# First layer of a two-layer mixture of experts: experts sorted on the chip by number of tokens, nine places of 128 slots and seven of 64

## The chip, the cores and the metric

The kernel runs on one core of a Trainium2 chip. The metric is the device time of one execution in microseconds (us); less is better. The engines of the core work side by side: TensorE (PE; its weight loads are PEld), VectorE (DVE), ScalarE (ACT), GpSimd (POOL) and SyncE (SP), and 16 DMA engines move data.

## The reference

Two layers over 256 latent and 256 context tokens of width 1024. Each layer has an attention part, which the change does not touch, and a mixture of 16 experts. The first layer runs it for all 512 tokens, the second for the 256 latent tokens. Every token picks one group of four experts and two experts in it:

```
grp = jnp.argmax(lg, -1)
le_sel = jnp.take_along_axis(le, grp[:, None, None], axis=1)[:, 0]
top_v, top_i = lax.top_k(le_sel, TOP_K)
w_top = jax.nn.softmax(top_v, -1) * p_grp
eid = grp[:, None] * EXPERTS_PER_GROUP + top_i
...
for e in range(N_EXPERTS):
    a = jax.nn.silu(hf @ w_gate[e]) * (hf @ w_up[e])
    y = y + gate[:, e:e + 1] * (a @ w_down[e]).astype(jnp.float32)
```

w_gate and w_up of one expert are 1024 x 512, w_down 512 x 1024, all float32: 6 MB per expert, 96 MB per layer. In the first layer 512 tokens make 1024 pairs of token and expert, 64 per expert on the mean.

## The kernel before

**First layer** (`full_experts`, lines 1318 to 1473). After the routing on VectorE (lines 1250 to 1317), `tables` (line 1328) makes for every expert the rows to gather, the rows to scatter and the weights of its 128 slots: VectorE compares the tokens' ranks with the slots' numbers (line 1336), TensorE multiplies with the tokens' records. `expert` (line 1373) gathers the rows from DRAM (`hfD`) by an indirect DMA of GpSimd (line 1376), turns them feature-major on TensorE (line 1386), and multiplies in three float32r passes: rows and weights are split into a high and a low part, and high x high, high x low and low x high are summed (`product`, lines 1369 to 1371). `split_w` (line 1353) splits the weights: ScalarE writes the high part (line 1358), VectorE, for one part in six GpSimd, the low part (line 1360), into ten buffers `hl`. The weighted output goes to `yD` in DRAM by an indirect DMA (line 1426), each token's two experts into two rows. Only the last expert's output stays in PSUM; `combine` and `finish` add it by a one-hot product (line 1672) to the rows of `yD`, which `base` reads back at the start of the second layer (lines 1640 and 1645).

The weights come in tiles of 1 MB, two each of gate, up and down per expert, through a ring of ten places (`RING[0]`), in the order of their use: `todo` (line 1149) holds up of expert e - 1, gate of e, down of e - 1. SyncE issues the loads (line 1135) in this order, each when its place is free. For a big tile that is after its split. Ten tiles are issued before the first split frees a place (`FILL`).

The loop (lines 1464 to 1472) lets the first half of the next expert's gate follow on up, and down follow on the next expert's gate. A scheduler orders the instructions of each engine from this. `overflow` (line 1609) runs further rounds for every expert if a flag says that one has more tokens than slots (line 1298).

**Second layer** (`half_experts`, from line 1475). Its experts have 64 slots. The products are plain float32, not split: a tile of weights goes from the ring straight to TensorE, the left half of the columns on one half of the array and the right half on the other (`ps[64 * t:64 * t + 64]`, lines 1547 and 1564).

Of the kernel before, what the change touches and what calls it, by code (L numbers as in the profile page):

```python
# [7 lines left out]
F32 = mybir.dt.float32  # L8
F32R = mybir.dt.float32r
BF16 = mybir.dt.bfloat16  # L10
# [10 lines left out]
E = 16  # L21
# [7 lines left out]
CAP = (128, 64)  # L29
RAW_A = 2  # L30
# [7 lines left out]
T4 = 6  # L38
LOG = (2, 3, 4, 5, 6, 7)

# column layout of the constant block (all of it follows from shapes alone)
C_ID, C_TRI, C_NAM, C_WIN, C_R64, C_R32, C_IOTA, C_TIE, C_COEF, C_TLOW, C_REV, C_IOTA2, C_END = np.cumsum(
    [0, 128, 128, 64, 256, 256, 128, 128, 4, 8, 1, 128, 128]).tolist()
# [15 lines left out]
def _constants():  # L59
# [15 lines left out]
    # slot records (valid, token in chunk, chunk, k, ...) -> row to gather, row to scatter, less BIG  # L75
    c[:, C_COEF:C_COEF + 8] = [-BIG, 1, 128, 0, -BIG, 1, 128, 512]
    c[:, C_TLOW] = p
# [4 lines left out]
def kern(tc, I, out):  # L82
# [23 lines left out]
    class Phase:  # L106
        """Working pool of a phase: its bytes are reused by the phases after it."""
# [24 lines left out]
    # ------------------------------------------------------------------ constants  # L132
# [9 lines left out]
    # records of the tokens of layer 0: valid, row, chunk, ..., 0; the rest comes with the routing  # L142
# [33 lines left out]
    def load_x():  # L176
        """residual streams: chunks 0, 1 latents, 2, 3 context"""
# [50 lines left out]
    def ln_stats(x):  # L228
        """-mean and 1 / std of the rows of x [128, D]"""
# [9 lines left out]
    def ln_stats2(x, total, tag):  # L239
        """the same where the row sums are there already"""  # L240
# [7 lines left out]
    def stats(x, c, tot, nmean, ss):  # L248
        """column c of -mean, and the sum of the squares about the mean"""
# [4 lines left out]
    def in_order(*engines):  # L254
        """what the block traces on these engines stays in this order"""
# [1503 lines left out]
```

## Time and profile before

| | |
|---|---|
| median of 3 runs | 1300.53 us (1297.07 to 1307.24) |
| span of the profiled execution, first to last instruction | 1302.6 us |
| mean granted TensorE clock, share of full speed | 0.926 |
| TensorE busy | 1146.7 us (88%) |
| VectorE busy | 793.7 us (61%) |
| ScalarE busy | 559.1 us (43%) |
| GpSimd busy | 254.3 us (20%) |
| moved by DMA | 315.77 MB, 242 GB/s on the mean |

No other time is given for the profiled execution; its span lies within the range of the three runs. The first layer's experts run from about 404 to 745 us, the second layer's from about 1046 to 1280 us. A busy TensorE is not TensorE at its peak, since a matmul's row ends later than the next one starts: the distance of starts is what one costs. A float32 product leaves two rows in the trace, a float32r product one.

### The profile page before, as it was taken

The page shows a single profiled execution, that of the slowest core. Times are in us where ns is not written, and L with a number is a line of the kernel's source. Part 1 is how long each engine was busy: PE and PEld are TensorE (multiplying, and loading weights), DVE is VectorE, ACT ScalarE, POOL GpSimd, SP SyncE. Part 2 cuts the span into 40 slices and gives each one's busy share as a digit, 9 for nine tenths or more (in the row PEclk, how much of TensorE's full clock was granted, in tenths as well). Part 3 has the DMA queues.
Part 4 walks back from the last instruction along what each step waited for, and adds up shares of the span by engine and source line. Part 5 has one row for each costly group of instructions (what it writes and reads, how often), then busy time and mean ns, then how long its engine had stood idle before and what let it go on. Part 6 is the DMA issues. An engine that isn't in the chain of part 4 may idle for free. (4 is left out here: it accounts for less than half of the span.)

```text
span 1302.6 us, 16444 instructions
## 1 busy us (share of the span) xinstructions
PE 1146.7 (88%) x5920; PEld 770.1 (59%) x5920; DVE 793.7 (61%) x1676; ACT 559.1 (43%) x951; POOL 254.3 (20%) x235
## 2 busy tenths in 40 slices
PE   5999999899945999989999978998989589999995
PEld 2777644367833777767777647654457455455552
DVE  4377156674797899979888688735874711211113
ACT  2332155664325677767677444415553311111110
POOL 0022011222132344435352205120001200000000
PEclk9999969989967899999999979997979789999998
DMA  9933546701567899999998453542723979999993
GB/s 351 311 106 83 188 171 236 241 12 34 202 226 250 284 328 346 336 330 352 307 319 276 175 176 119 153 162 106 259 84 101 329 244 395 393 394 394 394 394 138
DMA packets 151770, 315.77 MB, mean 242 GB/s; under 512 B 21295, under 2 KB 36405, under 8 KB 146560
## 3 DMA queue, kind: packets, MB, share of 16 engines
q1 hardware_dynamic: 146868, 305.96, 66.9%
q0 software_dynamic: 4560, 8.57, 1.8%
q8 instruction: 49, 0.80, 0.3%
q14 instruction: 41, 0.34, 0.1%
q10 hardware_dynamic: 252, 0.09, 0.0%
HBM read 307.28 MB, written 15.27 MB: 248 GB/s over the span
## 5 line engine op out<-in xcount | busy, mean ns | idle before, releaser
L1360 DVE TENSOR_TENSOR hl<-rb,hl 128x1024 fp32r<-128x1024 f32 x127 | 189.7, 1520 | 30.6 <-ACT hl L1358 30.3
L1358 ACT ACTIVATE hl<-rb 128x1024 fp32r<-128x1024 f32 x152 | 158.0, 1058 | 69.8 <-PE mm L1370 63.3
L1370 PE MATMUL mm<-hl,t 128*128 128x512 f32 x256 | 106.0, 414 | 3.2 <-DVE hl L1360 3.2
L1371 PE MATMUL mm<-hl,t 128*128 128x512 f32 x256 | 102.9, 402 | 4.5 <-DVE t L1389 4.3
L1369 PE MATMUL mm<-hl,t 128*128 128x512 f32 x256 | 103.0, 407 | 1.1 <-ACT t L1388 1.1
L1547 PE MATMUL mm<-rb,xt 128*64 128x256 f32 x816 | 101.0, 383 | 0.0
L563 PE MATMUL mm<-s,hh 128*128 128x512 f32 x216 | 88.1, 412 | 0.0
L565 PE MATMUL mm<-s,hh 128*128 128x512 f32 x216 | 87.9, 410 | 0.0
L564 PE MATMUL mm<-s,hh 128*128 128x512 f32 x216 | 87.0, 403 | 0.0
L1547 PEld LDWEIGHTS mm<-rb,xt 128*64 128x64 f32 x816 | 58.1, 137 | 35.3 <-issue 8.8
L1360 POOL TENSOR_TENSOR hl<-rb,hl 128x1024 fp32r<-128x1024 f32 x25 | 70.1, 2815 | 24.2 <-ACT hl L1358 23.5
L824 ACT ACTIVATE e<-mm,nmx 128x512 f32<-128x512 f32 (+1 forms) x96 | 58.4, 616 | 29.3 <-DVE nmx L819 16.3
L819 DVE TENSOR_REDUCE nmx<-mm 128x1 f32<-128x512 f32 (+1 forms) x80 | 52.7, 684 | 11.1 <-PE mm L813 10.3
L1371 PEld LDWEIGHTS mm<-hl,t 128*128 128x128 f32 x256 | 49.7, 194 | 16.2 <-DVE t L1389 6.7
L1370 PEld LDWEIGHTS mm<-hl,t 128*128 128x128 f32 x256 | 49.7, 194 | 14.7 <-DVE hl L1360 5.2
L1552 DVE TENSOR_TENSOR ta<-ta,mm 128x256 f32<-128x256 f32 x16 | 6.7, 421 | 84.4 <-ACT ta L1551 84.4
L1369 PEld LDWEIGHTS mm<-hl,t 128*128 128x128 f32 x256 | 49.7, 194 | 12.1 <-ACT t L1388 2.0
L1369 PE MATMUL mm<-hl,at 128*128 128x512 f32 x128 | 53.0, 414 | 3.7 <-ACT at L1408 3.7
L1371 PE MATMUL mm<-hl,at 128*128 128x512 f32 x128 | 50.2, 411 | 6.0 <-DVE at L1409 5.7
L833 POOL TENSOR_SCALAR e<-e,rc 128x256 f32<-128x256 f32 x32 | 30.0, 950 | 128.7 <-DVE rc L831 98.5
L1370 PE MATMUL mm<-hl,at 128*128 128x512 f32 x128 | 52.9, 413 | 1.5 <-DVE hl L1360 1.2
L424 ACT ACTIVATE s<-ra 128x1024 fp32r<-128x1024 f32 x30 | 31.3, 1059 | 51.4 <-PE mm L565 25.5
(494 smaller groups left out, 2437.4 us busy)
## 6 DMA issues: line engine op xcount, KB each, us to landing
rb<-in_moe_w_up_dram SPq DMA_DIRECT2D x52, 1024.0 KB
rb<-in_moe_w_down_dram SPq DMA_DIRECT2D x50, 1024.0 KB
rb<-in_moe_w_gate_dram SPq DMA_DIRECT2D x49, 1024.0 KB
ra<-in_w_ada_dram SPq DMA_DIRECT2D x40, 1024.0 KB
ra<-in_moe_w_gate_dram SPq DMA_DIRECT2D x14, 1024.0 KB
ra<-in_w_in_dram SPq DMA_DIRECT2D x24, 512.0 KB
ra<-in_moe_w_down_dram SPq DMA_DIRECT2D x11, 1024.0 KB
ra<-in_moe_w_up_dram SPq DMA_DIRECT2D x9, 1024.0 KB
```

Source lines behind the costliest of these rows:

```text
L424: S.activation(hi, w, AF.Copy)
L563: T.matmul(ps, a, hi[:, k2], start=k == 0, stop=False)
L564: T.matmul(ps, a, lo[:, k2], start=False, stop=False)
L565: T.matmul(ps, b, hi[:, k2], start=False, stop=k == KD - 1)
L819: V.tensor_reduce(nmx[:, :nb], ps, axis=AX, op=ALU.max, negate=True)
L824: S.activation(e[:, b], ps[:, b], AF.Exp, bias=nmx[:, b:b + 1], accum_out=sm[:, b:b + 1])
L1358: S.activation(hi, w[k2], AF.Copy)
L1360: eng.tensor_tensor(lo, w[k2], hi.bitcast(F32), op=ALU.subtract)
L1369: T.matmul(ps[:C], ah, hs[:, k2], start=first and k2 == 0, stop=False)
L1370: T.matmul(ps[:C], ah, ls[:, k2], start=False, stop=False)
L1371: T.matmul(ps[:C], al, hs[:, k2], start=False, stop=last and k2 == 1)
L1547: T.matmul(ps[64 * t:64 * t + 64, j], X[:, k, gi], wt, start=k == 0, stop=k == KD - 1)
```

## The change

The layer's experts 0 and 1 keep the first two places, so that their weights can be loaded before the routing is known. The other 14 are sorted on the chip by their number of tokens (`rank_experts`, `sort_experts`), and take the places 2 to 15. Places 0 to 8 run as before, with 128 slots in three passes. Places 9 to 15 have 64 slots and run as in the second layer, in float32 on the two halves of the array (`small_expert`). `ORDER` lets a big and a small place alternate: 0, 1, 2, 9, 3, 10, ..., 8, 15. SyncE reads the experts' numbers into registers, and the weights' addresses come from these. A small place's `down` is loaded in whole rows, its output is scattered in half rows of 512, and `tables` has a second set of constants for it. The flag for further rounds is also set if more than seven of the experts 2 to 15 have over 64 tokens. The buffers `t4` are five instead of six. The last place is small, so `combine` and `finish` work with one PSUM tile instead of two.

```diff
-T4 = 6
+N_FIRST, N_BIG = 2, 7
+ORDER = tuple(range(N_FIRST)) + tuple(s for i in range(N_BIG) for s in (N_FIRST + i, N_FIRST + N_BIG + i))
+T4 = 5
...
         def load_expert(e, n, i, late=False):
-            src = I[n][l, e] if isinstance(e, int) else I[n][l, ds(e, 1)].rearrange("a k n -> (a k) n")
-            if n == "moe_w_down" and half:
+            x = e if half or not isinstance(e, int) or e < N_FIRST else perm[e - N_FIRST]
+            src = I[n][l, x] if isinstance(x, int) else I[n][l, ds(x, 1)].rearrange("a k n -> (a k) n")
+            if n == "moe_w_down" and (half or small_slot(e)):
                 src, sh = src[256 * i:256 * i + 256], [128, 2, 1024]
...
+        order = range(E) if half else ORDER
...
-                    todo += [(e - d, f"moe_w_{n}", i) for i in range(2)]
+                    todo += [(order[e - d], f"moe_w_{n}", i) for i in range(2)]
+        def small_slot(e):
+            return isinstance(e, int) and e >= N_FIRST + N_BIG
...
+            V.tensor_scalar(over, ps[:, N_FIRST:E], float(C // 2), None, op0=ALU.is_gt)
+            S.activation(cnt, ps[:, :E], AF.Copy)
+            V.tensor_reduce(n64, over, axis=AX, op=ALU.add)
+            V.scalar_tensor_tensor(mxn, n64, float(C - N_BIG), mxn, op0=ALU.add, op1=ALU.max)
...
             def tables(cols, n, few=False):
...
+            def rank_experts(P):
+                key, rank = P([128, E]), P([128, E])
+                gt = PX("t2", [128, 512], bufs=2)[:, :E * E].rearrange("p (a b) -> p a b", a=E)
+                V.scalar_tensor_tensor(key, cnt, float(E), cst[:, C_KEY:C_KEY + E], op0=ALU.mult, op1=ALU.add)
+                V.tensor_tensor(gt, key[:, None, :].to_broadcast([128, E, E]),
+                                key[:, :, None].to_broadcast([128, E, E]), op=ALU.is_gt)
+                V.tensor_reduce(rank, gt, axis=AX, op=ALU.add)
+                return rank
+            def sort_experts():
+                rank = rank_experts(lambda sh: PX(nm('rk'), sh))
+                io = cst[:, C_IOTA:C_IOTA + E]
+                pf, pi = PX("pf", [1, E]), PX("pi", [1, E], I32)
+                eq = PX("t2", [128, 512], bufs=2)[0:1, :E * E].rearrange("p (a b) -> p a b", a=E)
+                V.tensor_tensor(eq, rank[0:1, None, :].to_broadcast([1, E, E]),
+                                io[0:1, :, None].to_broadcast([1, E, E]), op=ALU.is_equal)
+                V.tensor_tensor(eq, eq, io[0:1, None, :].to_broadcast([1, E, E]), op=ALU.mult)
+                V.tensor_reduce(pf, eq, axis=AX, op=ALU.add)
+                V.tensor_copy(pi, pf)
+                _, vals = nc.values_load_multi_w_load_instructions(
+                    pi[0:1, N_FIRST:E], engines=[mybir.EngineType.SP], min_val=0, max_val=E - 1,
+                perm.extend(vals)
+                wide = lambda a: a[:, :, None].to_broadcast([128, nch, E])
+                slots = io[:, None, :].to_broadcast([128, nch, E])
+                parts, t = [], R_(E)
+                for En in (E1, E2):
+                    pos, r, Es = R_(), R_(), R_(E)
+                    V.tensor_tensor(t, En, rank[:, None, :].to_broadcast([128, nch, E]), op=ALU.mult)
+                    V.tensor_reduce(pos, t, axis=AX, op=ALU.add)
+                    V.tensor_tensor(t, En, RK, op=ALU.mult)
+                    V.tensor_reduce(r, t, axis=AX, op=ALU.add)
+                    V.tensor_scalar(r, r, 1.0, None, op0=ALU.add)
+                    V.tensor_tensor(Es, slots, wide(pos), op=ALU.is_equal)
+                    parts.append((Es, r))
+                rks, gw = R_(E), R_(E)
+                (E1s, r1), (E2s, r2) = parts
+                V.tensor_tensor(rks, E1s, wide(r1), op=ALU.mult)
+                V.tensor_tensor(t, E2s, wide(r2), op=ALU.mult)
+                V.scalar_tensor_tensor(rks, rks, -1.0, t, op0=ALU.add, op1=ALU.add)
+                V.tensor_tensor(gw, E1s, wide(w1), op=ALU.mult)
+                V.tensor_tensor(t, E2s, wide(w2), op=ALU.mult)
+                V.tensor_tensor(gw, gw, t, op=ALU.add)
+                recs = R_(E, 8, dt=BF16)
+                G.tensor_copy(recs, rec)
+                records(recs, E2s, gw)
+                return rks, recs
...
+            def small_expert(tab, gi, e, xg):
+                idx, w, _, row = tab
+                h = C // 2
+                G.indirect_dma_start(out=xg[:h], out_offset=None, in_=hfD,
+                                     in_offset=bass.IndirectOffsetOnAxis(ap=idx[:h, gi, 0:1], axis=0),
+                X = PX("t4", [128, KD, 128], bufs=T4)[:, :, :h]
+                for kp in range(2):
+                    ps = tr([128, 4, 128])[:, :, :h]
+                    for k in range(4):
+                        T.transpose(ps[:, k], xg[:h, 128 * (4 * kp + k):128 * (4 * kp + k) + 128], ident[:h, :h])
+                    if kp == 0:
+                        S.activation(X[:, 0:4], ps, AF.Copy)
+                    else:
+                        V.tensor_copy(X[:, 4:8], ps)
+                ps = mm([128, 2, 256])
+                for j, n in enumerate(("moe_w_gate", "moe_w_up")):
+                    for kh in range(2):
+                        wt = weights(e, n, kh)
+                        for k in range(4):
+                            for t in range(2):
+                                T.matmul(ps[h * t:h * t + h, j], X[:, 4 * kh + k], wt[k // 2][:, k % 2, 256 * t:256 * t + 256],
+                                         start=kh + k == 0, stop=4 * kh + k == KD - 1)
+                        if j == 0:
+                            yield
+                a = PX("t2", [128, 512], bufs=2)[:, :256]
+                S.activation(a, ps[:, 0], AF.Silu)
+                V.tensor_tensor(a, a, ps[:, 1], op=ALU.mult)
+                yield
+                aT = PX("at", [128, 4, 128], bufs=4)[:, :2]
+                pt = tr([128, 2, 128])
+                for k in range(2):
+                    T.transpose(pt[:, k], a[:, 128 * k:128 * k + 128], ident)
+                S.activation(aT, pt, AF.Copy)
+                yield
+                ps = mxp.tile([128, 512], F32, name=nm("mx"), tag="mx")
+                for i in range(2):
+                    wt = weights(e, "moe_w_down", i)
+                    for k in range(2):
+                        for t in range(2):
+                            T.matmul(ps[h * t:h * t + h], aT[:, k, h * i:h * i + h], wt[k][:, 0, 512 * t:512 * t + 512],
+                                     start=i + k == 0, stop=i + k == 2)
+                if e == ORDER[-1]:
+                    final.extend((ps, w[:, gi:gi + 1], row[:, gi, 0:1]))
+                    return
+                y = PX("t4", [128, D], bufs=T4)[:, :512]
+                S.activation(y, ps, AF.Copy, scale=w[:, gi:gi + 1])
+                st = G.indirect_dma_start(out=yD.rearrange("n (t d) -> (n t) d", t=2),
+                                          out_offset=bass.IndirectOffsetOnAxis(ap=idx[:, gi, 1:2], axis=0),
+                for o in scat:
+                    tc.declare_no_dep(st.ins, o.ins, reason="an expert's rows are no other expert's")
+                scat.append(st)
...
+            def table(i):
+                s = ORDER[i]
+                if s in tabs:
+                    return tabs[s]
+                if s < N_FIRST:
+                    tabs[s] = tables(lambda i: (RK[:, :, s], rec[:, :, s]), 1), 0
+                    return tabs[s]
+                small = small_slot(s)
+                end = E if small else N_FIRST + N_BIG
+                n = min(3 if s in (N_FIRST, N_FIRST + N_BIG) else 4, end - s)
+                rks, recs = sorted_
+                t = tables(lambda i: (rks[:, :, s + i], recs[:, :, s + i]), n, small)
+                tabs.update((s + i, (t, i)) for i in range(n))
+                return tabs[s]
...
             fetch(FILL[0][4])
+            table(0)
+            table(1)
+            sorted_.extend(sort_experts())
             run = start(0)```

On SyncE, behind the branch of the further rounds, the weights' loads of the kernel before:

```order
L1135 DMA rb_3355<-in_moe_w_up_dram 128x4x512
L1135 DMA rb_3356<-in_moe_w_up_dram 128x4x512
L1135 DMA rb_3354<-in_moe_w_down_dram 128x4x512
L1135 DMA ra_3851<-in_moe_w_gate_dram 128x4x512
L1135 DMA ra_3873<-in_moe_w_gate_dram 128x4x512
L1135 DMA rb_3925<-in_moe_w_down_dram 128x4x512
```

and of the change (`pi` holds the experts' numbers):

```order
L1146 DMA rb_3355<-in_moe_w_up_dram 128x4x512
L1146 DMA rb_3356<-in_moe_w_up_dram 128x4x512
L1146 DMA rb_3354<-in_moe_w_down_dram 128x4x512
L1400 TENSOR_LOAD pi_3870
L1146 ISA
L1146 DMA ra_3964<-in_moe_w_gate_dram 128x4x512
L1146 ISA
L1146 DMA ra_3986<-in_moe_w_gate_dram 128x4x512
L1146 DMA rb_4047<-in_moe_w_down_dram 128x4x512
```

The read of the numbers stands ahead of the eleventh tile, and each load by a register has one instruction more.

On VectorE, ahead of the first expert (`oh` are the one-hot slots, `idx` the rows to gather, `hl` the splits of the weights, `t` the low part of the rows), before:

```order
L1336 TENSOR_SCALAR oh_3905<-cst,rt_810_3480 128x128 x4
L1343 TENSOR_REDUCE tf_3820<-ti_3817 128x2
L1345 TENSOR_SCALAR idx_3822<-tf_3820 128x2
L1360 TENSOR_TENSOR hl_3854<-ra_3347,hl_3853 128x1024
L1346 TENSOR_SCALAR tf_3820<-tf_3820 128x2
L1360 TENSOR_TENSOR hl_3858<-ra_3347,hl_3857 128x1024
L1360 TENSOR_TENSOR hl_3876<-ra_3348,hl_3875 128x1024
L1360 TENSOR_TENSOR hl_3928<-rb_3349,hl_3927 128x1024
L1389 TENSOR_TENSOR t_888_3835<-tr_3836,t_887_3834 128x512
```

and in the change, the stretch from the first index on:

```order
L1372 TENSOR_SCALAR idx_3838<-tf_3836 128x2
L1372 TENSOR_SCALAR idx_3858<-tf_3856 128x2
L1439 TENSOR_TENSOR hl_3967<-ra_3347,hl_3966 128x1024
L1397 TENSOR_TENSOR t_909_3871<-t_909_3871,cst 1x256
L1411 TENSOR_REDUCE rt_911_3906<-rt_910_3905 128x4
L1373 TENSOR_SCALAR tf_3836<-tf_3836 128x2
L1373 TENSOR_SCALAR tf_3856<-tf_3856 128x2
L1439 TENSOR_TENSOR hl_3971<-ra_3347,hl_3970 128x1024
L1398 TENSOR_REDUCE pf_3869<-t_909_3871 1x16
L1412 TENSOR_TENSOR rt_910_3905<-rt_804_3464,rt_810_3480 128x64
L1415 TENSOR_TENSOR rt_913_3908<-cst,rt_911_3906 128x64
L1439 TENSOR_TENSOR hl_3989<-ra_3348,hl_3988 128x1024
```

The sort lies between the first splits; the low part of the first rows comes 22 rows after the last one shown, behind the rest of the sort and the slots of the next table.

On TensorE, where the change's first small expert begins its gate (`mm_4494`, weights straight from `rb` and `ra`) while the big expert before it goes on to its down (`mm_4535`):

```order
L1518 MATMUL tr_4488<-cst,xg_826_3528 128x64 x2
L1529 MATMUL mm_4494<-rb_4168,t_1049_4481 64x256 x8
L1486 MATMUL tr_4507<-cst,t_1048_4475 128x128 x4
L1529 MATMUL mm_4494<-rb_4192,t_1049_4481 64x256 x8
L1529 MATMUL mm_4494<-ra_4325,t_1049_4481 64x256 x7
L1448 MATMUL mm_4535<-hl_4527,at_4505 128x512
L1449 MATMUL mm_4535<-hl_4528,at_4505 128x512
```

Products of half the array's width and of its full width alternate; their width changes 73 times from the first small expert to the last.

## Rows read from the trace of the kernel before

**Rows 1.** The page: TensorE's busy time; GB/s in 40 slices of 32.6 us.

```profile
PE 1146.7 (88%) x5920; PEld 770.1 (59%) x5920; DVE 793.7 (61%) x1676; ACT 559.1 (43%) x951; POOL 254.3 (20%) x235
...
GB/s 351 311 106 83 188 171 236 241 12 34 202 226 250 284 328 346 336 330 352 307 319 276 175 176 119 153 162 106 259 84 101 329 244 395 393 394 394 394 394 138
```

**Rows 2.** Stretches: length, busy us (instructions) of each engine, granted clock, DMA share, GB/s.

```profile
405.00:745.00 340.00, 310.51 (x1404) 244.10 (x1403) 292.55 (x322) 235.04 (x269) 130.03 (x61) 0.96 0.87 303
...
602.00:624.00 22.00, 20.49 (x97) 16.11 (x96) 19.80 (x23) 15.82 (x18) 7.57 (x3) 0.94 1.03 368
...
1100.00:1200.00 100.00, 97.03 (x685) 52.77 (x686) 19.07 (x39) 15.68 (x35) 0.00 (x0) 1.00 1.04 393
```

**Rows 3.** Who waited for whom, 405 to 745 us: us in total, times, longest.

```profile
ACT hl L1358 <- PE mm L1370: 77.9, 101, 4.1
...
SPq L1135 <- DVE hl L1360: 175.8, 77, 5.1
```

**Rows 4.** ScalarE's splits, 405 to 745 us: busy us, mean ns | idle before, releasers.

```profile
L1358 ACT ACTIVATE hl<-rb 128x1024 fp32r<-128x1024 f32 x151 | 157.0, 1058 | 69.8 <-PE mm L1370 63.3 <-POOL hl L1360 4.0 <-DMA rb<-in_moe_w_up_dram 1.5
```

**Rows 5.** TensorE in order of time, first layer: start, us, line, operation [idle before].

```profile
404.40 1.94 PE L1386 MATMUL tr<-cst,xg 128*128 128x128 f32 x8 [10.59 <-DMA xg<-hfD,idx]
...
407.19 0.63 PE L1369 MATMUL mm<-hl,t 128*128 128x512 f32 x1
407.62 0.63 PE L1370 MATMUL mm<-hl,t 128*128 128x512 f32 x1
...
412.67 0.39 PE L1369 MATMUL mm<-hl,t 128*128 128x512 f32 x1
412.90 0.39 PE L1370 MATMUL mm<-hl,t 128*128 128x512 f32 x1
...
433.24 0.60 PE L1386 MATMUL tr<-cst,xg 128*128 128x128 f32 x4
433.60 0.47 PE L1369 MATMUL mm<-hl,at 128*128 128x512 f32 x1
```

**Rows 6.** Line 1402, once per expert: durations in ns, first and last start in us.

```profile
L1402 DVE TENSOR_TENSOR t<-t,mm x16: 670/680/689, 420.5 to 735.7; 128x512 f32<-128x512 f32 x16
```

**Rows 7.** TensorE in order of time, second layer, one expert.

```profile
1069.45 3.62 PE L1547 MATMUL mm<-rb,xt 128*64 128x256 f32 x32
1072.90 3.60 PE L1564 MATMUL mx<-rb,at 128*64 128x512 f32 x16
1076.44 0.44 PE L1556 MATMUL tr<-cst,ta 128*128 128x128 f32 x2
1076.81 4.11 PE L1547 MATMUL mm<-rb,xt 128*64 128x256 f32 x36
```

**Rows 8.** The page: the loads' queue: packets, MB, share of 16 engines' span.

```profile
q1 hardware_dynamic: 146868, 305.96, 66.9%
```

**Rows 9.** VectorE in order of time, from the routing to the first rows.

```profile
387.16 0.22 DVE L1276 TENSOR_TENSOR rt<-rt,rt 128x64 f32<-128x64 f32 x1
...
394.48 0.86 DVE L1336 TENSOR_SCALAR oh<-cst,rt 128x128 bf16<-128x128 f32 x4
...
395.45 0.17 DVE L1345 TENSOR_SCALAR idx<-tf 128x2 int32<-128x2 f32 x1
...
406.16 0.69 DVE L1389 TENSOR_TENSOR t<-tr,t 128x512 fp32r<-128x512 f32 x1 [1.63 <-ACT t L1388]
```

**Rows 10.** SyncE's issues in order of time: start, us from first to last.

```profile
395.33 0.95 SPq L1135 DMA_DIRECT2D rb<-in_moe_w_up_dram  x2
...
400.14 3.71 SPq L1135 DMA_DIRECT2D ra<-in_moe_w_gate_dram  x2
...
732.65 1.77 SPq L1640 DMA_DIRECT2D hh<-yD  x4
```

**Rows 11.** GpSimd's last scatter, and TensorE where the second layer begins.

```profile
729.76 1.23 POOL L1426 DMA_INDIRECT yD<-t,idx  x1 [6.19 <-ACT hl L1358]
...
744.69 3.60 PE L1645 MATMUL mm<-hh,cst 128*128 128x512 f32 x8
```

More of the change, by code (lines that the diff above doesn't have):

```diff
@@ L1142, in load_expert @@
             return ws
-        ahead, todo = {}, []
+        ahead, todo, perm = {}, [], []
+        order = range(E) if half else ORDER
         for e in range(E + 1):
@@ L1296, in moe @@
         V.tensor_reduce(mxn, ps[:, :E], axis=AX, op=ALU.max)
+        if not half:
+            cnt, over, n64 = PX("cnt", [128, E]), PX("over", [128, E - N_FIRST]), PX("n64", [128, 1])
+            V.tensor_scalar(over, ps[:, N_FIRST:E], float(C // 2), None, op0=ALU.is_gt)
+            S.activation(cnt, ps[:, :E], AF.Copy)
+            V.tensor_reduce(n64, over, axis=AX, op=ALU.add)
+            V.scalar_tensor_tensor(mxn, n64, float(C - N_BIG), mxn, op0=ALU.add, op1=ALU.max)
         flag = PX("flag", [1, 1], I32)
@@ L1318, in full_experts, with records, tables @@
         def full_experts():
[L1320 to L1331 removed]
+            def records(rec, E2, Gw):
+                V.tensor_copy(rec[:, :, :, 3], E2)
+                for i in range(3):
+                    V.tensor_copy(rec[:, :, :, 4 + i], Gw)
+                    if i < 2:
+                        V.tensor_tensor(Gw, Gw, rec[:, :, :, 4 + i], op=ALU.subtract)
+            records(rec, E2, Gw)
+            def tables(cols, n, few=False):
+                c0, c1 = (C_IOTA2, C_COEF2) if few else (C_IOTA, C_COEF)
+                iota = cst[:, c0:c0 + 128]
+                co = cst[:, c1:c1 + 8].rearrange("p (a b) -> p a b", a=2)
+                tp = tr([128, 8, 8])[:, :n]
                 for i in range(n):
                     rkc, rc = cols(i)
[L1334 removed]
+                    oh = PX("oh", [128, nch, 128], BF16, bufs=2)
                     for ch in range(nch):
@@ L1441, in more, with spilled, start @@
                     pass
-            overflow([(RK, 1, F32), (rec.rearrange("p c e r -> p c (e r)"), 8, BF16)], more)
-            tabs = {}
-            def table(e):
-                if e not in tabs:
-                    n = {0: 1, 1: 1, 2: 2}.get(e, 4)
-                    t = tables(lambda i: (RK[:, :, e + i], rec[:, :, e + i]), n)
-                    tabs.update((e + i, (t, i)) for i in range(n))
-                return tabs[e]
-            def start(e):
-                t, i = table(e)
-                run = expert(t, i, e, xgs[e % 2])
+            def spilled():
+                rank = rank_experts(lambda sh: PX(nm("ro"), sh))
+                V.tensor_scalar(rank, rank, N_FIRST + N_BIG - 0.5, float(C // 2), op0=ALU.is_gt, op1=ALU.mult)
+                V.tensor_tensor(RKo, RK, rank[:, None, :].to_broadcast([128, nch, E]), op=ALU.add)
+            RKo = R_(E)
+            overflow([(RKo, 1, F32), (rec.rearrange("p c e r -> p c (e r)"), 8, BF16)], more, spilled)
+            tabs, sorted_ = {}, []
+            def table(i):
[12 more added lines that the diff above has]
+                return tabs[s]
+            def start(i):
+                t, gi = table(i)
+                run = (small_expert if small_slot(ORDER[i]) else expert)(t, gi, ORDER[i], xgs[i % 2])
                 with tc.issue_after(t[2]):
@@ L1461, in full_experts @@
             fetch(FILL[0][4])
+            table(0)
+            table(1)
+            sorted_.extend(sort_experts())
             run = start(0)
             next(run)
-            for e in range(E):
-                if e + 2 < E:
-                    table(e + 2)
+            for i in range(E):
+                if i + 2 < E:
+                    table(i + 2)
                 next(run)
-                then = start(e + 1) if e + 1 < E else iter((0, 0))
+                then = start(i + 1) if i + 1 < E else iter((0, 0))
                 next(run)
@@ L1607, in half_experts, with overflow @@
             return acc
-        def overflow(cols, more):
+        def overflow(cols, more, before=lambda: None):
             spill = []
@@ L1615, in overflow @@
             with tc.If(fv > 0):
+                before()
                 for dst, src, n, dt in spill:
```

62 lines of the change are left out of this document (26 added, 36 removed).

## The prediction

> **What bounds the kernel now.** I read the page's slices first, then the windows of the first layer's expert stage, then who waits there, then single rows. The page has TensorE busy for 88% of the span, and the memory rate lies between 276 and 352 GB/s in the slices that lie wholly in the first layer's experts (the 14th to the 22nd), but at 393 to 395 through the second layer's [rows 1]. So the second layer's stage runs at the rate of its weights, and the first layer's does not. From 405 to 745 us TensorE is busy 310.5 of 340 us, VectorE 292.6, and the memory moves 303 GB/s on the mean; one 22 us stretch inside reaches 368, and the second layer 393 [rows 2]. What ends the waits names the bound: ScalarE's splitting of the weights waits 77.9 us for matmuls to free its buffers [rows 3], and for weights, in the larger group of its rows, 1.5 us only [rows 4]; SyncE's loads wait 175.8 us for VectorE's splits, thus for free places in the ring [rows 3]. TensorE bounds this stage, VectorE is close behind, and the memory waits for both.
>
> One expert is 72 products (48 gate and up, 24 down) in three passes. At the higher clock they follow each other every 0.23 us, at the lower of the two levels every 0.43 us [rows 5]. 72 x 0.23 is 16.6 us; the stage's mean granted clock is 0.96 [rows 2]; with transposes and tables TensorE is busy 310.5 / 16 = 19.4 us per expert. The last products of the gate halves are 315.2 us apart over 15 experts, 21.0 us each [rows 6]; so 1.6 us per expert are idle.
>
> **The change, part by part.**
>
> *Seven experts become small.* The reference's own routing on its inputs gives experts 2 to 15 of the first layer 40, 35, 84, 110, 104, 108, 114, 63, 106, 99, 34, 21, 16, 21 tokens: exactly seven over 64, none over 128. So 9 places run as before, and 7 need 32 products of 256 columns and 8 of 512, in float32, two halves of the array side by side. The second layer does just this product: 32 records from start to start in 3.45 us, 0.108 each (36 in 4.11 us with the tail, 0.114), and 16 records of 512 columns in 3.54 us, 0.221 each [rows 7]. A float32 product leaves two records, so a small expert costs 64 x 0.115 = 7.4 us, with the larger value since rows of the two tiles alternate, and 16 x 0.221 = 3.5 us. Its ten transposes cost at most 0.19 us each (two in 0.37 us, [rows 7]) and at least 0.09 (four in 0.36 us, [rows 5]): 0.9 to 1.9, I take 1.4. With 0.3 for its table, 12.6 us. TensorE's work falls from 310.5 to 9 x 19.4 + 7 x 12.6 = 263 us.
>
> *Switching the array.* In the order below, small and big products alternate, and the column width changes 73 times in the stage. The row nearest is the second layer's pair of transposes between half-width products: 0.37 us [rows 7] where two would take 0.18 [rows 5], so 0.1 us a change. That gives 7 us; the lower end is nothing, since the 1.4 us for transposes may hold part of it. I take 4. The Trainium skill, in "TensorEngine Tiling (Array Packing)", Key Properties, says that a change of tiling mode drains the array, which speaks against alternating. It gives no price; a drain as long as one 512-column record would be an estimate of 16 us, and the time 1262. The row of the pair of transposes shows half of that a change.
>
> *Idle time.* Of the 29.5 us idle before, the big experts would keep 9/16, 17 us. But a small expert needs no split at all, so ScalarE and VectorE run ahead by the ten buffers meanwhile. I take 10; ends 5 and 20.
>
> *The weights.* The same 96 tiles of 1.049 MB are loaded, ten of them before the stage as now. 86 x 1.049 = 90.2 MB, and 1024 rows of 4 KB gathered and scattered are 8.4 MB: 98.6 MB. At 368 GB/s [rows 2] that is 268 us, at 393 [rows 2] 251. At the program's own mean per full use of the engines (305.96 MB in 66.9% of the span, [rows 8]) it is 351 GB/s, 281 us. Before, TensorE's 340 us covered it. Now TensorE needs 277, hardly more. The ring's ten tiles smooth pairs of a big and a small expert: 32 us of TensorE for 12 tiles, which take 12 x 1.049 / 368 = 34 us and gathers and scatters beside them.
>
> *Sorting.* It stands on VectorE ahead of the first experts. Both tables come first, then some 30 operations of the 128 x 64 kind, 0.22 us each [rows 9], laid between the first splits. Ahead of the first index stand two comparisons of 256 numbers, flags and a second set of table steps, some 12 operations: 3 us by that row, and the gather, which before was issued right behind its index at 395.45, is that much later. From that index to the rows' transposes at 404.40 [rows 5] are 9 us, and the rest of the sort fits into it only in part (18 x 0.22 and eight comparisons of 0.215 us [rows 9], 6 us; VectorE idled 1.63 us ahead of the rows' low part, at 406.16): that part comes 4 to 5 us later. I charge 4, ends 2 and 8. Behind VectorE's sort stands SyncE: it reads the experts' numbers ahead of the eleventh tile, issued at 400.14 before [rows 10]. The ring's last three tiles, issued from 395.33 on [rows 10], take 8 us at 393 GB/s, so a restart at 405 instead of 400 idles the memory about 2 us. GpSimd copies the records ahead of the first gather, but they are complete before the tables begin, some 4 us before the index: nothing; without that cover the gather waits for it. Each later load has one more instruction on SyncE; its pairs of issues are 0.95 us where no place is waited for [rows 10], a tile takes 2.8 us at 368 GB/s, so up to 2 us per load are covered, and each microsecond beyond costs 86.
>
> *The end.* The last expert is now small. Before, the last scatter was issued at 729.76 [rows 11], the rows were read back from 732.65 [rows 10], and the sums began at 744.69 [rows 11]: 14.9 us, hidden by the last expert's work. Now some 6 us of products follow the second last expert. The chain needs at least 2.9 us to the read and 2.1 MB / 393 = 5.3 us for it, and 2 us of the output's copies stand before: 10 to 17 us, of which 4 to 11 are exposed. I take 8.
>
> **The sum.** Before, the stage starts at 404.4 [rows 5] and the sums begin at 744.7. After: 404.4 + 4 + 263 + 4 + 10 + 8 = 693.4. The memory's own path ends at 402 + 268 + 6 = 676, and takes over at 98.6 MB in 277 us, below 356 GB/s. The stage is 51 us shorter, 1302.6 becomes 1251. All else keeps its order. The profiled span is 2.1 us over the median, so 1250 us.
>
> **The rivals.**
>
> 1. *The weights become the bound, at the rate of now.* For: the engines' share is 0.87 over the stage [rows 2] though only 303 GB/s move, so 303 / 0.87 = 348 at full share. Against: 368 and 393 in the other rows. At 340 to 320 GB/s the path ends at 402 + 290 to 308 + 6, with 8 at the end and 5 of stalls 711 to 729: 1267 to 1285 us.
>
> 2. *TensorE stays dense.* 18.8 us per big expert, 12.0 per small, 5 idle, no switching cost, 2 at the start, 5 at the end: 404.4 + 2 + 169 + 84 + 5 + 5 = 669: 1226 us.
>
> 3. *Slower: the clock falls.* Its place is the stretch of pairs. TensorE in order waits there for a tile of weights that no split buffers any more, and after an idle stretch its clock is at the lower level: every 0.43 us after the 10 us wait for the first gather [rows 5]. At 1.2 GHz a pair takes 64 us, seven pairs 448, two first experts 42: the stage ends near 900, 1455 us. Break-even is 7 x 32 / c + 42 + 16 = 340, a mean granted clock c of 0.79 in the pairs. Against: the second layer waits for weights too and keeps 1.00 [rows 2].
>
> 4. *The change does not do what it says.* With an eighth expert over 64 tokens every expert gets three further rounds, 48 x 21 = 1008 us more, 2300 us. Expert 9 has 63 tokens, so two tokens would have to move.
>
> **How the numbers follow.** My forecast has 0.60 (1238 to 1266). Rival 1 has 0.20, rival 2 0.09, rival 3 0.04, rival 4 0.02; 0.05 is left for a cost per load over 3 us on SyncE and the like, which would give 1290 and more. Less than 1% (13 us) can't be told from no change. Faster is 0.60 + 0.09 and all of rival 1 but what reaches 1288, 0.89 in all; the same 0.05; slower 0.06. The range takes in most of both: 1228 to 1276.
>
> **What would show it.** Right: small products of 0.115 and 0.22 us per record; a pair of experts every 33 to 35 us; memory over 350 GB/s from 450 us on; SyncE's loads still waiting for places; sums starting near 693. The first gather 3 us later. Wrong: TensorE waiting for tiles of weights at under 350 GB/s (rival 1), a granted clock under 0.9 in the pairs (rival 3), the loops of further rounds in the trace (rival 4), or a last scatter that is not waited for.

## The result, and the profile after

The changed kernel takes 1262.72 us (median of 4, 1259.04 to 1267.17) against 1301.68 (median of 4): a ratio of 0.9708, 95% interval 0.9666 to 0.975. Measured once more beside other versions it was 0.9712 (0.9678 to 0.9746). The forecast was 1250 us, its range 1228 to 1276.

The profiled execution took 1259.04 us. The page, its TensorE row and the GB/s of 40 slices, against [rows 1]:

```profile
PE 1104.7 (88%) x5962; PEld 701.2 (56%) x5962; DVE 670.7 (53%) x1619; ACT 464.3 (37%) x860; POOL 203.8 (16%) x222
...
GB/s 351 317 128 82 199 182 259 234 9 1 243 159 232 256 325 377 387 376 385 389 384 196 286 121 121 193 121 162 233 51 192 302 311 394 394 393 393 394 394 122
```

Stretches, columns as in [rows 2]: the whole stage from the first rows' transposes to the base sums, its part to the first small place's activation, and from there to the last one's.

```profile
400.10:702.20 302.10, 275.42 (x1443) 180.90 (x1443) 169.19 (x249) 140.85 (x177) 76.82 (x46) 0.96 0.92 332
400.10:482.30 82.20, 73.27 (x358) 54.66 (x359) 65.51 (x110) 48.53 (x56) 24.55 (x13) 0.91 0.89 297
482.30:695.40 213.10, 197.86 (x1067) 124.89 (x1066) 101.75 (x136) 91.24 (x119) 52.10 (x34) 0.98 0.94 349
```

The stage went from 340.3 us (404.40 to 744.69, [rows 5, 11]) to 302.2. TensorE's busy time in it fell from 310.8 to 275.4 us, and 26.7 us were idle. VectorE is at 56%. The rest of the program hardly moved: from the base sums to the end it was 557.9 us before and 554.9 after.

The rows once per place, against [rows 6]: nine big ones and seven small.

```profile
L1481 DVE TENSOR_TENSOR t<-t,mm x9: 673/686/689, 419.8 to 680.2; 128x512 f32<-128x512 f32 x9
...
L1535 DVE TENSOR_TENSOR t<-t,mm x7: 408/420/420, 482.3 to 695.4; 128x256 f32<-128x256 f32 x7
```

From 482.3 to 695.4 there are six pairs: 35.5 us each on the mean (31.3 to 38.6), where 33 to 35 were forecast. A pair's 12 tiles and 1 MB of rows are 13.6 MB, 384 GB/s at that pace, near the second layer's 394. So the memory looked like the bound. But the loads run out in the last pair, and that pair is the longest. The first and the last 35.5 us of the pairs:

```profile
482.30:517.80 35.50, 34.91 (x188) 22.74 (x188) 16.51 (x20) 15.50 (x20) 9.80 (x7) 1.00 1.03 381
659.90:695.40 35.50, 30.26 (x151) 17.81 (x149) 12.28 (x13) 10.79 (x14) 6.58 (x4) 0.95 0.46 175
```

And TensorE's waits in the stage name no load (the row left out on top is the wait that ends with the stage's start):

```profile
...
PE mm L1450 <- DVE t L1468: 6.7, 5, 2.3
PE mm L1448 <- ACT t L1467: 3.9, 5, 1.8
PE mm L1449 <- DVE hl L1439: 3.3, 5, 0.8
PE mm L1449 <- POOL hl L1439: 3.2, 3, 1.3
PE mm L1448 <- ACT hl L1437: 2.0, 1, 2.0
...
```

(TensorE, tile and line, whom it waits for: us in total, times, longest.)

What such a wait looks like, in order of time. TensorE: a small place's down, and the next big place's products behind it.

```profile
665.80 1.94 PE L1548 MATMUL mx<-rb,at 128*64 128x512 f32 x8
669.75 0.50 PE L1448 MATMUL mm<-hl,t 128*128 128x512 f32 x1 [2.01 <-ACT hl L1437]
671.01 0.80 PE L1449 MATMUL mm<-hl,t 128*128 128x512 f32 x1 [0.76 <-DVE hl L1439]
671.60 0.63 PE L1450 MATMUL mm<-hl,t 128*128 128x512 f32 x1
672.03 0.63 PE L1448 MATMUL mm<-hl,t 128*128 128x512 f32 x1
...
674.47 0.39 PE L1448 MATMUL mm<-hl,t 128*128 128x512 f32 x1
674.69 0.39 PE L1449 MATMUL mm<-hl,t 128*128 128x512 f32 x1
```

ScalarE in the same stretch:

```profile
665.91 0.60 ACT L1480 ACTIVATE t<-mm 128x512 f32<-128x512 f32 x1 [6.04 <-PE mm L1450]
667.79 0.69 ACT L1554 ACTIVATE t<-mx,tw 128x512 f32<-128x512 f32 x1 [1.28 <-PE mx L1548]
668.37 0.38 ACT L1520 ACTIVATE t<-tr 128x256 f32<-128x256 f32 x1
668.64 3.89 ACT L1437 ACTIVATE hl<-rb 128x1024 fp32r<-128x1024 f32 x4
```

ScalarE stood idle for 6.04 us, copied what TensorE had just finished, and only then (668.64) split the tile that TensorE needed next. TensorE waited 2.01 and 0.76 us, and its next products follow each other every 0.43 us, the lower level, until 674.2. Over the whole stage ScalarE's longest wait is for a big place's turned activations, which it copies; its splits wait for buffers, and for no load:

```profile
ACT at L1487 <- PE tr L1486: 39.0, 8, 9.2
ACT hl L1437 <- PE mm L1449: 37.3, 35, 5.6
...
```

### The profile page after: what moved, and what is told of

The parts are those of the page before. It is cut to its first block, busy times and chain, and to the rows that moved or that the text cites. A ratio compares the mean times of both kernels' runs of the same rounds, so it can differ in the third digit from the quotient of the medians.

```text
span 1257.2 us, 16382 instructions
## 1 busy us (share of the span) xinstructions
PE 1104.7 (88%) x5962; PEld 701.2 (56%) x5962; DVE 670.7 (53%) x1619; ACT 464.3 (37%) x860; POOL 203.8 (16%) x222
## 5 line engine op out<-in xcount | busy, mean ns | idle before, releaser
L1439 DVE TENSOR_TENSOR hl<-rb,hl 128x1024 fp32r<-128x1024 f32 x71 | 90.7, 1302 | 58.5 <-ACT hl L1437 58.5
L1437 ACT ACTIVATE hl<-rb 128x1024 fp32r<-128x1024 f32 x84 | 85.8, 1054 | 34.1 <-PE mm L1449 34.0
L1694 PEld LDWEIGHTS mm<-rb,xt 128*64 128x64 f32 x816 | 58.5, 137 | 35.5 <-issue 9.0
L1448 PE MATMUL mm<-hl,t 128*128 128x512 f32 x144 | 61.7, 428 | 5.9 <-ACT t L1467 3.9
L1450 PE MATMUL mm<-hl,t 128*128 128x512 f32 x144 | 60.0, 419 | 6.7 <-DVE t L1468 6.7
L1449 PE MATMUL mm<-hl,t 128*128 128x512 f32 x144 | 61.7, 429 | 2.9 <-DVE hl L1439 2.7
L875 PE MATMUL tr<-cst,e 128*128 128x128 f32 x256 | 44.9, 307 | 4.0 <-DVE e L843 1.4
L573 PEld LDWEIGHTS mm<-s,hh 128*128 128x128 f32 x216 | 40.9, 190 | 13.5 <-issue 3.1
L575 PEld LDWEIGHTS mm<-s,hh 128*128 128x128 f32 x216 | 40.9, 189 | 13.2 <-issue 3.2
L574 PEld LDWEIGHTS mm<-s,hh 128*128 128x128 f32 x216 | 41.0, 190 | 12.3 <-issue 2.6
L1711 PE MATMUL mx<-rb,at 128*64 128x512 f32 x192 | 47.4, 597 | 0.0
L875 PEld LDWEIGHTS tr<-cst,e 128*128 128x128 f32 x256 | 31.9, 154 | 26.8 <-issue 14.5
L321 PE MATMUL mm<-ra,cT 128*32 128x512 f32 x320 | 43.5, 603 | 3.4 <-DMA ra<-in_w_ada_dram 3.4
```

The source lines that it names most:

```text
L573: T.matmul(ps, a, hi[:, k2], start=k == 0, stop=False)
L574: T.matmul(ps, a, lo[:, k2], start=False, stop=False)
L575: T.matmul(ps, b, hi[:, k2], start=False, stop=k == KD - 1)
L875: T.transpose(tp[:, k2, 128 * c:128 * c + 128], probs[hh][c][:, 0, 128 * kt:128 * kt + 128], ident)
L1437: S.activation(hi, w[k2], AF.Copy)
L1439: eng.tensor_tensor(lo, w[k2], hi.bitcast(F32), op=ALU.subtract)
```

## The experiments

Whole times carry several microseconds that are not the change's: the last store of rows ahead of the stage fell between 378.1 and 388.8 us in these profiles. The stage itself (first rows' transposes to base sums) repeats: 302.2, 302.6 and 301.4 us in three profiles of the changed kernel's order; each of the other stages stands on one profile. So stages are compared; "changes" counts the changes of the array's width that the written program has on TensorE there (rows' transposes of small places not counted; 74 with the one into the first small product, which the prediction's 73 leave out).

| run | changes | stage us | TensorE busy | ratio to before |
|---|---|---|---|---|
| changed kernel | 74 | 302.2 | 275.4 | 0.9708 (0.9666 to 0.975) |
| e1 half tiles | 68 | 286.9 | 269.3 | 0.9642 (0.9594 to 0.969) |
| e2 half products | 68 | 298.0 | 257.7 | 0.9727 (0.969 to 0.9765) |
| e3 no sort | 70 | 303.4 | 276.3 | 0.9748 (0.971 to 0.9787) |
| e4 blocks | 24 | 295.0 | 263.5 | 0.9636 (0.9601 to 0.9671) |
| e5 early order | 68 | 295.1 | 272.3 | 0.9658 (0.961 to 0.9707) |
| e6 late order, half tiles | 74 | 302.2 | 275.1 | 0.9726 (0.9678 to 0.9774) |
| e7 same order | 74 | 302.6 | 275.7 | 0.9685 (0.9638 to 0.9732) |
| e8 small early | 70 | 297.4 | 275.0 | 0.9696 (0.9632 to 0.9759) |
| e9 mixed | 70 | 292.3 | 271.5 | 0.9631 (0.9564 to 0.9698) |
| e10 blocks, early order | 26 | 297.6 | 267.2 | 0.9715 (0.9653 to 0.9776) |
| e11 twos | 52 | 309.7 | 275.8 | 0.9747 (0.9713 to 0.9781) |
| e12 changed kernel again | 74 | 301.4 | 274.7 | 0.9712 (0.9678 to 0.9746) |

**e1, half tiles.**

```diff
+                if small_slot(e):
+                    SY.dma_start(wt[:, :h], src[:, :h])
+                    return [wt[:, :h], wt[:, :h]]
                 SY.dma_start(wt, src)
```

> Left out: every tile of a small place is loaded by half (0.5 MB instead of 1 MB), and both halves of its products use the half that is there; TensorE's, VectorE's and ScalarE's instructions are the same. A pair of a big and a small place took 35.5 us in the changed kernel's trace, at 384 GB/s and a DMA share of 1.03. Theory W (the memory bounds the pairs): a pair moves 10.5 MB instead of 13.6, 27 us at 384 GB/s, so TensorE's 33.5 us decide: pairs of 33.5 to 34, the stage 12 us shorter, about 1248 us. Theory T (TensorE with its order and changes of width bounds the pairs, the memory only keeps step): pairs stay at 35 to 35.5 us, the memory falls to about 300 GB/s, 1257 to 1264 us.

Pairs of 33.95 us, the stage 15.3 us shorter: it looks like W. But the scheduler, which writes the engines' order when the kernel is built, had written another order too. ScalarE's, late in the stage (S a split with the times it follows; x, a and y a big place's rows' copies, copies of turned activations and outputs, X, A and Y a small place's; G a big place's activation, g a small one's):

```
changed kernel   yxxg S1 A S3 G S1 YX S4 a S3 yxx S1 g S2 A S1 GYX S5 a S3 ygA
half tiles       y S2 gxx S2 A S3 GYX S3 a S2 y S2 gxx S2 A S3 GYX S2 aygA
```

In the last pair, from g on, with half tiles five splits (S2, S3) stand ahead of G, Y and X and two behind them; with whole tiles three stand ahead and five behind these copies, which wait for TensorE. So e1 changed two things.

**e2, half products.**

```diff
-                        for k in range(4):
+                        for k in (0, 3):
```

> Left out: half of the gate and up products of each small place (32 of 64 records, 3.7 us at 0.117), with all loads kept. Theory W: pairs stay at 35 to 35.5 us, since 13.6 MB at 384 GB/s take that long, and the time stays at 1257 to 1264 us. Theory T: a pair falls to about 32 us, the stage by up to 25 us, about 1236 us.

TensorE's busy time fell by 17.7 us, the stage by 4.2. The six pairs took 36.5 us on the mean, longer than with the products left in, where T had 32 and W 35 to 35.5. That spoke against T, but here, too, the order was written anew, with splits later still ("GYX S6 a"), and TensorE waited 5.6 us for ScalarE's splits and 11.7 for VectorE's. It decides nothing between W and O.

**e3, no sort.**

```diff
...
-            sorted_.extend(sort_experts())
+            perm.extend([8, 5, 7, 10, 6, 11, 4, 9, 2, 3, 12, 13, 15, 14])
```

> Left out: the sort. The order of the experts that the sort finds for these inputs is written into the program, so weights' addresses are constants, SyncE reads no register, and the tables come straight from the routing's ranks. This prices the sort. The prediction's charge (4 us at the start, and 2 us of memory idle that lie within it): 1254 to 1257 us, the first rows 3 to 4 us earlier, pairs of 35.5 us as they are. Rival: the instructions that form addresses on SyncE, or VectorE's sort between the first splits, cost more than that: the stretch from the first rows to the first pair (82 us) is 8 us or more shorter, or pairs are shorter by 1 us or more, 1250 us or less.

The first three big places and the first small one took 78.6 us from the first rows, against 82.2: 3.6 us, near the prediction's charge. The first rows came 20.6 us behind the last store, against 20.2 with the sort. Later in the stage, whose order is written anew here too, these 3.6 us are lost again (pairs of 36.3 us on the mean, where 35.5 were expected), so taking the sort out won nothing in the whole: 303.4 us, and a time of 1265.8 where 1254 to 1257 were expected. The rival (8 us or more) fell.

**e4, blocks.**

```diff
-ORDER = tuple(range(N_FIRST)) + tuple(s for i in range(N_BIG) for s in (N_FIRST + i, N_FIRST + N_BIG + i))
+ORDER = tuple(range(E))
```

> Only the order of the places changes: 0 to 8 (128 slots), then 9 to 15 (64 slots), no alternation, so the array changes its width some 15 times instead of 73. Theory W (memory bound where small places run): the big places take 21 us each at 300 GB/s, 189 us; the small ones 6.8 MB each at 384 GB/s, 17.7 us, less 27 us that the full ring of ten tiles gives: 98 us; with 8 at the end 295 us for the stage against 302, about 1252 us. Theory T: small places of 12.6 us as TensorE needs, 189 + 88 + 8 = 285 us, about 1242 us. Rival: the ring can't be kept ahead, the alternation is what carries the memory, and small places take over 18 us each: 189 + 126 + 8 = 323 us, about 1280 us.

295.0 us, W's number (T had 285), in an order that is again newly written; 24 changes of width, where some 15 were expected. Its interval lies below that of e12. Stretches of the big and of the small places (the ninth big place's down lies in the second, the last small one's behind it), and two of the small places' waits for loads (9.6 us in all):

```profile
406.20:594.00 187.80, 169.96 (x771) 134.32 (x772) 166.27 (x215) 127.62 (x145) 72.29 (x35) 0.94 0.92 326
...
594.00:695.00 101.00, 89.42 (x658) 48.06 (x656) 12.75 (x35) 14.55 (x30) 12.69 (x13) 1.00 1.02 374
...
PE mm L1529 <- DMA rb<-in_moe_w_up_dram: 3.1, 4, 0.8
PE mm L1529 <- DMA rb<-in_moe_w_gate_dram: 2.9, 3, 1.4
```

In a row, small places do wait for the memory. And the same products keep TensorE busy for 263.5 us instead of 275.4, with 50 changes of width fewer.

**e5, e6, e7: bytes and order apart.** Each engine's instructions of the stage are chained in a written order by edges that bind the order of issue and add no wait: e5 whole tiles in e1's order, e6 half tiles in the changed kernel's order, e7 whole tiles in their own.

```diff
...
+            traced = nc.cur_bb.bb.instructions[n0:]
+            for text in ORDERS.values():
...
+                for before, ins in zip(run, run[1:]):
+                    tc.add_manual_dep(ins, before.name, mybir.DependencyInfo(
+                        mybir.DependencyClass.NoSync, mybir.DependencyReason.DATA), reason="order")
```

> The changed kernel with all its loads whole, but each engine's instructions in the first layer's experts stand in the order that the scheduler wrote for the kernel with half tiles (e1): ScalarE's splits come two or three earlier against its copies that wait for TensorE. Theory O (the written order bounds the pairs: ScalarE reaches a big place's splits only behind copies that wait for TensorE, and TensorE then waits for the splits; the scheduler wrote it so because it plans with slower loads): pairs fall from 35.5 to 34 to 34.6 us (13.6 MB at the second layer's 394 GB/s), the stage from 302 to about 290 us, 1246 to 1250 us. Theory W (the memory bounds them at 384 GB/s): pairs stay at 35.5 us, the stage at 300 us or more, 1257 to 1264 us.

> Left out: as in e1 each tile of a small place is loaded by half and used twice. Each engine's order is that of the changed kernel with whole tiles. Theory O: pairs stay near 35.5 us although the memory moves 23% less, the stage at about 300 us, 1256 us or more. Theory W: pairs fall to 33.5 to 34 us as in e1, the stage to about 288 us, 1247 us.

> Control for the two: the changed kernel with its own order written down in the way that e5 and e6 have theirs; nothing else differs from it. Both theories: pairs of 35.5 us, stage of 302 us, 1257 to 1264 us. If it differs by more than 4 us in the stage, writing the order down is itself a change, and e5 and e6 are to be read against this run.

e7 and e6, the whole stage:

```profile
398.15:700.79 302.64, 275.72 (x1444) 181.08 (x1444) 169.36 (x251) 140.92 (x177) 76.81 (x46) 0.96 0.91 332
```

```profile
408.08:710.30 302.22, 275.05 (x1444) 180.83 (x1444) 169.56 (x252) 140.84 (x177) 77.08 (x47) 0.96 0.75 260
```

260 GB/s instead of 332, and the same stage, place by place within 0.5 us. So the memory did not bound the changed kernel, although its share was 1.02 to 1.04 in five of the six pairs. W fell for this order. e5, the whole stage, and ScalarE's largest waits from 483 to 693 us (its lines are 48 higher, L1485 is the split):

```profile
405.00:700.10 295.10, 272.29 (x1443) 182.61 (x1443) 171.89 (x249) 143.11 (x177) 79.79 (x46) 0.96 0.93 338
```

```profile
ACT hl L1485 <- PE mm L1497: 45.5, 35, 5.6
...
ACT hl L1485 <- DMA rb<-in_moe_w_gate_dram: 8.3, 2, 5.8
...
ACT hl L1485 <- DMA rb<-in_moe_w_down_dram: 5.1, 2, 4.1
```

The order alone takes 7.5 us off (e5 against e7), 7.0 of them behind the seventh big place's activation. It is the order of all engines together; ScalarE's was not changed by itself. ScalarE's splits now mostly wait for full buffers, as before the change [rows 3], and here they do wait for loads, 18.6 us over four kinds of tile. Of O's forecast only a part came: 295.1 us for the stage, where O had 290 and W 300 or more; pairs of 35.3 us on the mean and a time of 1258.0, as W had them; and the whole times' intervals of e5 and e7 overlap. Orders and bytes together tell why:

| stage, us | whole tiles | half tiles |
|---|---|---|
| changed kernel's order | 302.6 (e7) | 302.2 (e6) |
| early order | 295.1 (e5) | 286.9 (e1) |

In the changed kernel's order the fewer bytes take nothing off, in the early one 8.2 us. So the order binds the changed kernel, and the memory comes right behind it.

**e8 to e11: other orders of the places**, all but the order as e5.

```diff
+ORDER = (0, 1, 9, 2, 10, 3, 11, 4, 12, 5, 13, 6, 14, 7, 8, 15)  # e8
+ORDER = (0, 1, 9, 2, 10, 3, 4, 11, 5, 12, 6, 13, 7, 14, 8, 15)  # e9
+ORDER = tuple(range(E))                                          # e10
+ORDER = (0, 1, 9, 10, 2, 3, 11, 12, 4, 5, 13, 14, 6, 7, 8, 15)  # e11
```

> As e5 (full loads, each engine's order planned with half tiles and written down), and the places run in the order 0, 1, 9, 2, 10, 3, 11, 4, 12, 5, 13, 6, 14, 7, 8, 15: the first small place comes third, so the three big places at the start, in which the memory moved some 300 GB/s, are not in a row. Theory M (after e5 the memory bounds the pairs, and what it left unused in the first 80 us is missing at the end): the stage falls from e5's 295 to 285 to 289 us, 1246 to 1250 us. Theory T (TensorE's sum with its changes of width and its waits bounds the whole stage): the sum is the same, 294 to 297 us, 1256 to 1259 us.

> As e8 with the order 0, 1, 9, 2, 10, 3, 4, 11, 5, 12, 6, 13, 7, 14, 8, 15: the third big place that was moved away from the start stands in the middle, where the ring of tiles can fill again. Theory M: like e8 or up to 3 us better, stage 284 to 288 us, 1245 to 1249 us. Theory T: 294 to 297 us, as e8.

> As e4 (nine big places, then seven small), with each engine's order planned with half tiles and written down. e4's stage was 295 us, its small places waited 9.6 us for weights on the chip. Theory M: the small block runs at 17.7 us per place less what the ring holds, the ring can't hold more, so 293 to 296 us, 1250 to 1253 us. Theory O alone (the written order binds there too): the big block gets 5 us or more shorter, 290 us or less, 1247 us or less.

> As e5 (full loads, order planned with half tiles and written down), the places in the order 0, 1, 9, 10, 2, 3, 11, 12, 4, 5, 13, 14, 6, 7, 8, 15: two small places, then two big ones. The array changes its width 52 times instead of 70 in e9; at 0.12 us a change (0.09 into a small product, 0.15 back, from the distances of starts in the changed kernel) that is 2 us. Theory S (the changes of width and the waits for splits are what is left above TensorE's bare work): 288 to 291 us for the stage, 1247 to 1250 us. Theory M (the memory has to be fed evenly; two small places take 13.6 MB in 25 us of TensorE, which the ring can't carry): 295 to 300 us, 1255 us or more.

e8 came out 0.4 us above T's range for the stage, e9 between the two theories. In e11 TensorE and ScalarE waited for loads (TensorE's 16.8 us are rows' copies that stand behind such splits on ScalarE):

```profile
PE mm L1577 <- ACT t L1568: 16.8, 3, 9.6
```

```profile
ACT hl L1485 <- DMA rb<-in_moe_w_gate_dram: 19.8, 3, 12.3
ACT hl L1485 <- DMA ra<-in_moe_w_gate_dram: 14.4, 2, 12.8
ACT hl L1485 <- DMA rb<-in_moe_w_up_dram: 13.8, 2, 8.0
```

So S fell: with ten tiles and two small places in a row, the next big place's splits wait for loads, and 309.7 us lie beyond M's range as well. e10's stage is 1.6 us over M's range and 2.6 over e4's: an order planned with half tiles does no good there. (Its whole time lies further off, since 562.8 us follow its stage, 7.9 more than in the changed kernel.)

> The changed kernel itself, unaltered, on the same chip as e11, so that versions are compared with it and not with its times elsewhere. All theories: ratio 0.967 to 0.972, stage 302 us.

As expected. Of the versions, e4 is faster than the changed kernel by intervals that do not touch (0.9601 to 0.9671 against 0.9678 to 0.9746; the changed kernel's first interval, from 0.9666 on, just touches). e9 has the shortest stage of those that leave nothing out of the experts, 292.3 us, but its interval (0.9564 to 0.9698) overlaps.

## Why the prediction was right, and where it was not

The mechanism held: TensorE with its waits for splits and copies, and not the memory (e6), set the stage, seven small experts took 35 us off its busy time, and no further rounds ran. The gain was 39 us instead of 51. From the last store to the base sums the forecast had 18.9 + 4 + 263 + 4 + 10 + 8 = 307.9 us; the trace has 379.91 to 702.28, 322.4. Of the 14.5 us between them 8.4 are TensorE's busy time and 6.0 its idle time. That the time fell near the forecast owes something to luck: the end was charged 5 us too much, which hides part of two terms that were too small. Step by step:

*Small products.* Right. 16 records of 256 columns with the way back to a big product take 1.88 us (below), and 16 of 512 columns 3.65 (the last place's, below); in e4 the seven small places' transposes and products were busy 86.3 us, 12.3 each, and 12.3 were charged without the tables.

*Switching the array.* This is the term that failed: 4 us, at most 7, against some 13.

```profile
676.53 0.39 PE L1448 MATMUL mm<-hl,t 128*128 128x512 f32 x1
676.85 1.95 PE L1529 MATMUL mm<-rb,t 128*64 128x256 f32 x16
678.73 0.50 PE L1449 MATMUL mm<-hl,t 128*128 128x512 f32 x1
679.07 0.40 PE L1450 MATMUL mm<-hl,t 128*128 128x512 f32 x1
679.30 0.39 PE L1448 MATMUL mm<-hl,t 128*128 128x512 f32 x1
```

The big product ahead of a change costs 0.32 instead of 0.23 us; 16 small records 1.88 instead of 1.73 (0.108 each, [rows 7]); the first big product behind them 0.34 instead of 0.23. That is 0.35 us there and back, 0.17 a change, 13 us for 74. (Nineteen times in the stage a run of 256 columns follows a big product, 0.32 us behind its start in the median.) The prediction had taken its price from a pair of transposes between half-width products and had none of these three places. TensorE's busy time agrees: 275.4 us where 263 + 4 were forecast. So does e4: 50 changes fewer are 8.8 us by this price, and its busy time was 11.9 lower, in an order that differs in more than that. Busy time does not follow the changes alone: e11 has 22 fewer and is busy 0.4 us longer, at a granted clock of 0.92 instead of 0.96. No run changes the number of changes by itself. The Trainium skill's rule in "TensorEngine Tiling (Array Packing)", Key Properties, that a change of mode drains the array, agrees in kind; the estimate of 16 us drawn from it was nearer than the value taken. That its 1262 us is the time measured is in part chance, since idle time was off too.

*Idle time.* 26.7 us in the stage, where 20.7 were left for it (10, 8 at the end, and what of the sort's 4 lies behind the first rows); ahead of the end it was 23.7 against 12.7. It was expected that ScalarE and VectorE run ahead by their ten buffers. They could not: the order written for ScalarE puts a big place's splits behind copies that wait for TensorE. e5 against e7 prices the order at 7.5 us: 4.1 of idle time and 3.4 of busy time, of which six changes of width fewer are 1.0. That the scheduler writes splits late because it plans with slower loads than the chip's is inferred from e1, where fewer bytes alone moved them forward; its plan itself is not shown.

*Sorting.* 4 us were charged, 3.6 found (e3, with the reserve on its order). The first big place's activation came 4.9 us later than before against the last store (39.9 us instead of 35.0). The first rows came only 1.3 us later than before against the last store (20.2 instead of 18.9; the gather was forecast 3 us later), and their low part cost TensorE 2.24 us:

```profile
406.18 0.80 PE L1450 MATMUL mm<-hl,t 128*128 128x512 f32 x1 [2.24 <-DVE t L1468]
```

SyncE's read of the experts' numbers held the eleventh tile up more than charged: issued 12.1 us behind the last three tiles of the ring, where it was 4.8 before [rows 10] and 5 more were forecast.

```profile
390.90 0.94 SPq L1146 DMA_DIRECT2D rb<-in_moe_w_up_dram  x2
...
403.04 1.04 SPq L1146 DMA_DIRECT2D ra<-in_moe_w_gate_dram  x2
```

No wait of TensorE or ScalarE for a load shows from the first rows to the first small place's activation, so that it cost more there does not show. Address instructions on SyncE cost nothing that shows.

*The end.* 8 us were charged, 3 found. The last scatter, the read and the sums follow in 7.7 us (14.9 before, [rows 10, 11]), and the last small place's own 3.6 us of down cover most of it:

```profile
694.58 0.98 POOL L1500 DMA_INDIRECT yD<-t,idx  x1 [7.87 <-DVE t L1499]
...
697.85 3.41 SPq L1788 DMA_DIRECT2D hh<-yD  x4
...
696.77 3.65 PE L1548 MATMUL mx<-rb,at 128*64 128x512 f32 x16 [0.47 <-ACT at L1541]
701.99 0.36 PE L162 MATMUL mx<-rec 1*128 1x480 bf16 x1 [1.57 <-DVE vbc L1805]
```

*The rivals.* The memory moved 375 to 389 GB/s in five of the six pairs, not 320 to 340, and was not the bound (e6); but it is the next one (e1 against e5, e11). By the prediction's own sum it would have taken over below 346 GB/s (98.6 MB in the 285 us from 402 to 687), not 356. Dense TensorE failed by the changes of width and by idle time, 26.7 us where it had some 10. The clock in the pairs was 0.98, so the slower rival's condition was far off; but its mechanism is there on a small scale, after waits for splits instead of tiles, as the rows from 669.75 us show.

## What to carry to other kernels

Price an alternation of array widths at every place where it shows: before, within and behind the short run. Where a scheduler writes the order, an experiment that changes bytes or work can change the order as well (e1, e2, e3): write the order down and change one at a time, before calling the memory or an engine the bound. A memory at full share is no proof of a memory bound; the test is whether fewer bytes in the same order make the stage shorter.

## What the hardware showed that was not expected

- The cast of the 16 sorted numbers to integers, which stands in the chain to SyncE's read, took 2.30 us. The cast itself is short: in e1 it took 0.16 us. In the changed kernel a split of GpSimd was under way, and the cast ended with it (399.83 and 399.80). In e1 no such split runs beside the cast, and there an operation of the sort took 2.06 us up to the end of one. In all eleven profiles with the long cast it ends within 0.03 us of GpSimd's split. So the long time is a wait for GpSimd's split; no run shows why VectorE waits for it.

```profile
395.81 3.99 POOL L1439 TENSOR_TENSOR hl<-ra,hl 128x1024 fp32r<-128x1024 f32 x1 [0.79 <-ACT hl L1437]
...
397.53 2.30 DVE L1399 CAST pi<-pf 1x16 int32<-1x16 f32 x1
```

and in e1:

```profile
404.53 2.35 POOL L1442 TENSOR_TENSOR hl<-ra,hl 128x1024 fp32r<-128x1024 f32 x1 [0.72 <-ACT hl L1440]
...
404.90 2.06 DVE L1415 TENSOR_TENSOR rt<-rt,rt 128x64 f32<-128x64 f32 x1
...
408.15 0.16 DVE L1402 CAST pi<-pf 1x16 int32<-1x16 f32 x1
```

- The DMA share stays at 0.91 and 0.92 over the stage with whole tiles and 0.75 with half ones, for the same 302 us: a share near 1 says that transfers are always under way, not that somebody waits for them.
